# A two-block transformer kernel on one core: one ring of four for all weight halves, context low halves on VectorE, one rounding step on ScalarE

## The chip, the cores and the metric

The kernel runs on one core of a Trainium2 chip, as one program. The metric is the device time of one execution in microseconds; the value before is the median of three runs. The engines are named as in the profile: PE is TensorE (matmuls), DVE is VectorE, ACT is ScalarE, POOL is GpSimd, SP is the engine that issues most of the loads.

## The reference, cut to what matters

Batch 1, 256 tokens, width 1024, all in float32. Two blocks follow each other; the first has two layers, the second one layer.

```python
def reference(x, ...):
    x = first_block(x, ...)      # RWKV-7 mix, SwiGLU; differential attention, SwiGLU
    return second_block(x, ...)  # modulated token mixer, convolutional FFN, final norm

def second_block(x, c, ctx, c_ctx, w_ada, ...):
    ada = silu(c) @ w_ada + b_ada ; ada_c = silu(c_ctx) @ w_ada + b_ada
    hc = modulate(rmsnorm(ctx, norm_mix), csh1, csc1)
    logf_f, k_f, logf_b, k_b, vc = hgrn2_gates(hc @ w_in[:, :3 * w], ...)
    hf_c = advance_state(h0, k_f, vc, ...) ; hb_c = advance_state(h0, flip(k_b), flip(vc), ...)
    h = modulate(rmsnorm(x, norm_mix), sh1, sc1)
    o = token_mixers(h @ w_in, ..., hf_c, hb_c)       # two gated scans and a gMLP branch
    x = x + g1 * (o @ w_out)
    h2 = modulate(rmsnorm(x, norm_ffn), sh2, sc2)
    x = x + g2 * conv_ffn(h2, w_up, taps, conv_b, w_down, rows)   # a * gelu(conv3x3(g))
    return rmsnorm(x, norm_final)
```

The context `ctx` (256 more tokens) is used only for the two start states `hf_c` and `hb_c` of the scans. Three slices of `w_in` are applied to it: the values (`w_iv` in the kernel) and the two gates (`w_cf`, `w_cb`).

## The kernel before, in words

**Products in three parts.** Every large product is made of rounded float32 operands: a value is split into a high half `hi` (the value rounded) and a low half `lo` (what the rounding left), for weights and activations alike. `mm3` then issues three matmuls for each tile, high by high, high by low and low by high. So every weight chunk of 128 rows by 1024 columns is loaded (`raw`, a ring of `NRAW` = 5 buffers, issued by SP), rounded on ACT (`S.copy`, L276) and subtracted (`sub`, L273) before TensorE may use it.

**`stream`** (L279) does that for one chunk. Its `eng` chooses who subtracts: VectorE where nothing is given, GpSimd where `G` is given; with `"dma"` ACT writes the rounded value (L285) and its negative (L286), and a DMA that GpSimd issues (L287) adds the weight from memory onto it. Its `ring` chooses the buffers of the two halves. The usual ring is that of the pool `wp` with `NHI` = 3 pairs, so the rounding of a chunk waits until TensorE is through with the chunk three places earlier in that ring.

**`ptm`** (L377) multiplies tokens by a weight in four chunks of 256 rows each, for both halves of the tokens; `pfm` makes the product with channels on the partitions. The stages, in the order of the program, are: the RWKV projections with a chain over four groups of heads (`p`, `G1`; the time-shifted keys' weight `w_k` is streamed with `"dma"`); the output projection `w_o`; a first feed-forward (`ffn`, 22 steps); key, query and value projections (`pj`); attention in six groups of heads (`heads_a`: scores `sc`, maximum `c_mx`, exponentials `pe`; `heads_b`: the combination of the two softmaxes in `pe`, its transposes `tr`, the product with the values `po`; `heads_c`: the norm of each head and `oT`); the context (below); the attention's output `w_ao`; a second feed-forward; the token mixer (`mh`, gates with `logsig`, eight weights through `pfm` and `ptm`, levels of the scan); `w_out`; and the convolutional feed-forward.

**The context** is normalised in two halves of 128 tokens: the half is loaded into `crow` (a DMA that ACT issues, L1043), its squares are summed on ACT (`sq`, L330), and it is transposed on TensorE by a scaled identity `dg` into a bank `p`, from which `gr`, `chh` and `chl` are made. Then `w_iv` and `w_cf` (beside the attention) and `w_cb` (after `w_ao`) are applied with `ptm`; these three have `lambda m: G`, so GpSimd makes their twelve low halves. The two loads of `ctx` use the same buffer one after the other: in the order of the program the second DMA waits for the last transpose of the first half.

**The mixer's projections** `w_vm`, `w_u`, `w_iv`, `w_ga` are one call of `ptm` with sixteen chunks m. Even chunks have their low half from VectorE and use the ring of three; odd chunks use `"dma"` and a ring `x` of two pairs of their own (tiles `xhi`, `xlo`), so that an odd chunk waits for the chunk four places earlier, an even one for the chunk six places earlier.

**The feed-forward** (`ffn`, L812) prepares the activation of each step in `post`: the hook makes `act`, L833 rounds it to `acth` on VectorE, and `sub` makes `actl` there. The convolutional one (`conv_hook`) uses eight VectorE instructions a step for the taps (L1304), a Gelu on ACT (L1306) and a product (L1307).

**The order of the work** is not that of the text. The whole program is built under `tile.TileContext(nc, schedule_with_timeline_sim=True)` (L1333): a scheduler that imitates the engines' times chooses the order of the instructions on every engine, each of which then runs strictly in its order. Any edit can therefore move instructions far from it.

## Time and profile before

| | us |
|---|---|
| median of three runs | 1212.76 (1209.64 to 1217.07) |
| the profiled execution | 1209.02, its span 1206.9 |
| PE busy | 1113.0, 92% of the span |
| DVE busy | 858.0, 71% |
| ACT busy | 632.5, 52% |
| POOL busy | 194.4, 16% |

The span is the time from the first to the last instruction of the profiled execution; 2.1 us lie around it. Busy time counts the union of an engine's instructions. A busy share is a mean over stages that have different limits: in the three feed-forwards TensorE is busy all the time, in the stages between them it waits. The granted clock of TensorE is given as a share of full speed, so 0.50 is the lower of its two levels (1.2 against 2.4 GHz).

### The profile page before, as it was taken

Reading aid. Unit: us, or ns where it says so; the run is one execution under the profiler, and the core shown is the slowest. Engines: PE = TensorE matmul, PEld = TensorE weight load, DVE = VectorE, ACT = ScalarE, POOL = GpSimd, SP = SyncE. Lnnn points to the kernel's source line nnn. Section 1 sums busy time; section 2 is a strip of 40 time slices with the busy share of each in tenths; the row PEclk is TensorE's granted clock in tenths of the full one; section 3 lists DMA queues with packets and bytes.
Section 4 is the critical chain, followed back from the end, with each engine's and each line's share of the span. In section 5 each row is a group of like instructions: output and inputs, shape, how many; then the busy total and the mean of one; then the engine's idle time right before and its main releaser. Section 6 shows DMA issues by size and latency. Waiting matters only on the chain.

```text
span 1206.9 us, 19872 instructions
## 1 busy us (share of the span) xinstructions
PE 1113.0 (92%) x7788; PEld 975.2 (81%) x7788; DVE 858.0 (71%) x1508; ACT 632.5 (52%) x1042; POOL 194.4 (16%) x156
## 2 busy tenths in 40 slices
PE   4999999779999999998999999999898789999995
PEld 4788549669999998886679999998876669999994
DVE  5687756859997566856659887554667667877787
ACT  6976145445434346757658334444867446344451
POOL 2242301200000001243130000004001112232320
PEclk8989878889999999999999999999989899999998
DMA  5354220248888563544147997662667234555551
GB/s 191 129 133 129 71 62 32 88 146 278 291 271 310 193 210 103 182 158 139 35 158 261 343 329 251 186 209 81 200 183 195 53 122 138 183 185 188 179 158 53
DMA packets 56589, 205.40 MB, mean 170 GB/s; under 512 B 6288, under 2 KB 6800, under 8 KB 56496
## 3 DMA queue, kind: packets, MB, share of 16 engines
q1 hardware_dynamic: 52128, 189.82, 47.0%
q0 software_dynamic: 2016, 7.34, 3.5%
q10 hardware_dynamic: 2352, 6.98, 1.7%
q8 instruction: 61, 1.00, 0.3%
q14 instruction: 32, 0.26, 0.1%
HBM read 203.06 MB, written 1.05 MB: 169 GB/s over the span
## 4 chain that ended last, share of the span: by engine, by line
PE 74%; DVE 12%; ACT 6%; DMA 5%; issue 2%; POOL 1%; POOLq 0%; ACTq 0%; DVEq 0%
PE p L298 31%; PE tr L298 16%; PE acc L298 14%; PE pj L298 6%; PE sc L298 3%; DVE lo L273 1%; DMA raw<-in_dn 1%; PE W L298 1%; ACT hi L276 1%; PE tr L310 1%; PE G L298 1%; PE px L298 1%; DVE cacc L1304 1%; DVE lo L655 1%; DVE lo L657 1%
## 5 line engine op out<-in xcount | busy, mean ns | idle before, releaser
L276 ACT CAST hi<-raw 128x1024 fp32r<-128x1024 f32 x198 | 205.9, 1047 | 153.9 <-PE p L298 84.1
L273 DVE TENSOR_TENSOR lo<-raw,hi 128x1024 fp32r<-128x1024 f32 x162 | 201.9, 1251 | 83.1 <-ACT hi L276 82.9
L298 PE MATMUL p<-fhh,hi 128*128 128x256 f32 x576 | 164.5, 286 | 2.5 <-ACT fhh L276 1.7
L298 PE MATMUL p<-fhl,hi 128*128 128x256 f32 x576 | 165.0, 286 | 1.2 <-DVE fhl L362 0.9
L298 PE MATMUL p<-fhh,lo 128*128 128x256 f32 x576 | 163.9, 285 | 0.0
L276 ACT CAST dhi<-raw 128x1024 fp32r<-128x1024 f32 x66 | 69.2, 1049 | 133.0 <-DMA raw<-in_dn 133.0
L298 PE MATMUL tr<-fhh,hi 128*128 128x256 f32 x480 | 136.0, 284 | 0.0
L298 PE MATMUL tr<-fhl,hi 128*128 128x256 f32 x480 | 135.9, 283 | 0.0
L298 PE MATMUL tr<-fhh,lo 128*128 128x256 f32 x480 | 135.7, 283 | 0.0
L273 DVE TENSOR_TENSOR dlo<-raw,dhi 128x1024 fp32r<-128x1024 f32 x66 | 83.6, 1267 | 56.7 <-ACT dhi L276 56.7
L273 POOL TENSOR_TENSOR lo<-raw,hi 128x1024 fp32r<-128x1024 f32 x36 | 87.8, 2441 | 189.4 <-ACT hi L276 186.0
L298 PEld LDWEIGHTS p<-fhh,hi 128*128 128x128 f32 x576 | 111.4, 193 | 4.5 <-ACT fhh L276 1.9
L298 PEld LDWEIGHTS p<-fhl,hi 128*128 128x128 f32 x576 | 111.3, 193 | 3.5 <-DVE fhl L362 1.7
L298 PEld LDWEIGHTS p<-fhh,lo 128*128 128x128 f32 x576 | 111.3, 193 | 0.3 <-issue 0.2
L298 PE MATMUL acc<-dhi,acth 128*128 128x512 f32 x264 | 103.6, 392 | 1.3 <-DVE acth L833 1.3
L298 PE MATMUL acc<-dlo,acth 128*128 128x512 f32 x264 | 103.4, 392 | 0.0
L298 PE MATMUL acc<-dhi,actl 128*128 128x512 f32 x264 | 100.7, 390 | 1.0 <-DVE actl L273 1.0
L317 POOL TENSOR_TENSOR s_rstd<-s_ms,mhalf 128x1 f32<-128x1 f32 (+2 forms) x32 | 34.8, 1091 | 361.5 <-DVE s_ms L331 272.4
L298 PEld LDWEIGHTS tr<-fhh,hi 128*128 128x128 f32 x480 | 91.9, 192 | 1.2 <-issue 0.2
L298 PEld LDWEIGHTS tr<-fhl,hi 128*128 128x128 f32 x480 | 91.9, 192 | 1.2 <-issue 0.2
L298 PEld LDWEIGHTS tr<-fhh,lo 128*128 128x128 f32 x480 | 91.9, 192 | 0.0
L888 DVE CUSTOM_DVE_ANT_0 junk<-wada,crow 128x1024 f32<-128x1024 f32 x64 | 78.0, 1219 | 8.9 <-DMA wada<-in_w_ada 7.3
(452 smaller groups left out, 2518.5 us busy)
## 6 DMA issues: line engine op xcount, KB each, us to landing
raw<-in_gu SPq DMA_DIRECT2D x132, 512.0 KB, 4.4
raw<-in_dn SPq DMA_DIRECT2D x66, 512.0 KB, 4.4
wada<-in_w_ada SPq DMA_DIRECT2D x48, 512.0 KB, 5.1
raw<-in_w_r SPq DMA_DIRECT2D x8, 512.0 KB, 4.4
raw<-in_w_k SPq DMA_DIRECT2D x8, 512.0 KB, 3.8
raw<-in_w_v SPq DMA_DIRECT2D x8, 512.0 KB, 4.7
raw<-in_w_o SPq DMA_DIRECT2D x8, 512.0 KB, 4.5
raw<-in_w_ak SPq DMA_DIRECT2D x8, 512.0 KB, 4.4
```

The costliest lines, as they stand in the source:

```text
L273: (eng or V).tensor_tensor(out=out, in0=raw, in1=hi.bitcast(F32), op=ALU.subtract)
L276: S.copy(hi, raw)
L298: PE.matmul(out, lhsT=l, rhs=r, start=start, stop=stop, skip_group_check=True)
L310: PE.transpose(o, s_, ident)
L317: G.tensor_tensor(out=r, in0=ms, in1=mhalf[:, :n], op=ALU.pow)
L655: V.tensor_tensor(out=tmp[:, s + 1:, 0:s], in0=bc(Ab[:, s + 1:, s:s + 1], shp), in1=bc(Tb[:, s:s + 1, 0:s], shp), op=ALU.mult)
L657: V.tensor_tensor(out=Tb[:, s + 1:, 0:s], in0=Tb[:, s + 1:, 0:s], in1=tmp[:, s + 1:, 0:s], op=ALU.add)
L888: V.tensor_tensor_reduce(out=junk, in0=raw, in1=src, scale=1.0, scalar=0.0, op0=ALU.mult, op1=ALU.add, accum_out=dst[:, e:e + 1])
L1304: V.scalar_tensor_tensor(out=a4[:, ro, co], in0=g4[:, ri, ci], scalar=taps[:, fb, k:k + 1], in1=a4[:, ro, co], op0=ALU.mult, op1=ALU.add)
```

## The change

`NHI` becomes 4. The ring of four then serves all chunks of the mixer's projections too: the separate ring `x` and the callable form of `ring` are gone, so that every chunk, odd or even, waits for the chunk four places earlier. The three context products lose their `lambda m: G`, which makes VectorE the subtracting engine. In the convolutional feed-forward the rounding of `act` into `acth` is done by ACT, in the two others still by VectorE.

```diff
-NHI = 3
+NHI = 4
...
-        rp, tag, n = ring(i) if callable(ring) else ring or (wp, "", NHI)
+        rp, tag, n = ring or (wp, "", NHI)
...
-            V.tensor_copy(ah, raw)
+            (S.copy if hook is conv_hook else V.tensor_copy)(ah, raw)
...
+    conv_hook = None
...
-    ptm([(a["w_iv"], 0, lambda t, ps: S.copy(cv[:, t * 512:(t + 1) * 512], ps))], ch, 0, lambda m: G)
+    ptm([(a["w_iv"], 0, lambda t, ps: S.copy(cv[:, t * 512:(t + 1) * 512], ps))], ch, 0)
...
-        ptm([(w, 0, got.__setitem__)], ch, 0, lambda m: G, acc_bank=acc_bank)
+        ptm([(w, 0, got.__setitem__)], ch, 0, acc_bank=acc_bank)
...
-        eng=lambda m: "dma" if m % 2 else V, ring=lambda i: (MX, "x", 2) if i % 2 else (wp, "", NHI))
+        eng=lambda m: "dma" if m % 2 else V)
```

The line numbers after L861 are two higher in the changed kernel. Since the scheduler makes the order, the edit shows itself in many places of the engines' queues. Three of them follow.

ACT, where the second half of the context is loaded (`crow_5541`; `pj`, `qsq` and the `hi` of L292 belong to the key, query and value projections). Before:

```order
L292 ACTIVATE hi_4721<-raw_4719,cst_67 128x512 x2
L1043 DMA crow_5541<-in_ctx 128x1024
L330 ACTIVATE sq_5543,s_ss_5544<-crow_5541 128x512
L292 ACTIVATE hi_4736<-raw_4734,cst_67 128x512 x2
L276 CAST chh_5501<-gr_5534 128x4x128
L330 ACTIVATE sq_5543,s_ss_5544<-crow_5541 128x512
L932 ACTIVATE qsq_4655<-pj_4566 128x512
```

Changed (L956 became L958; `pe_5154` and `pe_5155` are the first exponentials of the attention):

```order
L954 ACTIVATE av_4462<-pj_5094,rx_4424 128x512
L958 ACT_TABLE_LOAD
L276 CAST hi_5635<-raw_5633 128x1024
L356 ACTIVATE gr_5522<-p_5517,adc_2280,gm_2281 128x128 x4
L1045 DMA crow_5541<-in_ctx 128x1024
L330 ACTIVATE sq_5543,s_ss_5544<-crow_5541 128x512
L276 CAST chh_5500<-gr_5522 128x4x128
L276 CAST chh_5501<-gr_5534 128x4x128
L330 ACTIVATE sq_5543,s_ss_5544<-crow_5541 128x512
L980 ACTIVATE pe_5154,c_se_5151<-sc_5148,c_mx_5150 128x128 x4
L980 ACTIVATE pe_5155,c_se_5151<-sc_5149,c_mx_5150 128x128 x4
```

The second half's load stood in the middle of the projections; now it stands behind them, directly ahead of the attention's first exponentials.

PE, the start of the attention (`sc` are the scores, `tr_5213` the first transposes of `pe`; `p_5583`, `p_5590` and `p_5661` are context projections, `p_5553` and `p_5565` transposes of the context). Before, the end of that piece:

```order
L298 MATMUL p_5590<-hi_5635,chl_5503 128x512
L298 MATMUL p_5590<-hi_5635,chh_5501 128x512
L298 MATMUL p_5590<-lo_5636,chh_5501 128x512
L298 MATMUL sc_5177<-kT_4458,qT_4460 128x128 x4
L298 MATMUL sc_5178<-kT_4458,qT_4460 128x128 x4
L310 MATMUL tr_5213<-cst_67,pe_5154 128x128 x4
L298 MATMUL p_5590<-hi_5635,chl_5503 128x512
L298 MATMUL p_5661<-hi_5657,chh_5500 128x512
```

Changed:

```order
L298 MATMUL pj_5094<-hi_5103,xnl_4395 128x512
L298 MATMUL p_5517<-dg_5515,crow_5505 128x128
L298 MATMUL p_5529<-dg_5515,crow_5505 128x128 x4
L298 MATMUL sc_5148<-kT_4457,qT_4459 128x128 x4
L298 MATMUL sc_5149<-kT_4457,qT_4459 128x128 x4
L298 MATMUL sc_5177<-kT_4458,qT_4460 128x128 x4
L298 MATMUL p_5553<-dg_5551,crow_5541 128x128 x4
L298 MATMUL p_5565<-dg_5551,crow_5541 128x128 x4
L298 MATMUL sc_5178<-kT_4458,qT_4460 128x128 x4
L310 MATMUL tr_5213<-cst_67,pe_5154 128x128 x4
L298 MATMUL p_5583<-hi_5579,chh_5500 128x512
```

Before, 47 of the 48 matmuls of the first context product stood between the end of the projections and `tr_5213`; now none does, and thirteen of the sixteen transposes of the context stand behind the projections.

ACT in the mixer, around the last of the four `logsig` chains (`ls_8486`; `hi_8558` and `hi_8588` are chunks of `w_q`, 9026 and 9058 the first two odd chunks, `hi_9013` the first even one). Before:

```order
L285 CAST xhi_9026<-raw_9024 128x1024
L276 CAST hi_8558<-raw_8556 128x1024
L1031 ACTIVATE ls_8486<-p_8425 128x512
L286 ACTIVATE xlo_9027<-xhi_9026 128x1024
L1036 ACTIVATE kb_8215<-ls_8418 128x512
L1032 ACTIVATE ls_8486<-ls_8486 128x512
L285 CAST xhi_9058<-raw_9056 128x1024
L276 CAST hi_8588<-raw_8586 128x1024
L1033 ACTIVATE ls_8486<-ls_8486 128x512
L286 ACTIVATE xlo_9059<-xhi_9058 128x1024
```

Changed:

```order
L276 CAST hi_8588<-raw_8586 128x1024
L1033 ACTIVATE ls_8486<-p_8425 128x512
L1234 COPY grow_9331<-sp_9374 128x512
L1034 ACTIVATE ls_8486<-ls_8486 128x512
L1035 ACTIVATE ls_8486<-ls_8486 128x512
L276 CAST hi_9013<-raw_9011 128x1024
L1137 ACTIVATE qe_8660<-gb_8214 128x512
L1038 ACTIVATE kb_8215<-ls_8486 128x512
L285 CAST hi_9026<-raw_9024 128x1024
L1132 COPY ke_8659<-kf_8213 128x512
L1114 COPY qc_8216<-p_8493 128x512
L1133 COPY ke_8659<-kb_8215 128x512
```

The odd chunks' copies stood between the steps of the chain; now the chain comes first and the odd chunks follow it.

## Rows read from the trace of the kernel before

**Rows 1.** The page, engines: busy us (share of the span) and instructions.

```profile
PE 1113.0 (92%) x7788; PEld 975.2 (81%) x7788; DVE 858.0 (71%) x1508; ACT 632.5 (52%) x1042; POOL 194.4 (16%) x156
```

**Rows 2.** Windows by stage: length, busy us of each engine, PEclk, DMA share, GB/s.

```profile
534.00:560.00 26.00, 24.12 (x125) 18.99 (x124) 13.55 (x23) 17.66 (x52) 16.28 (x7) 1.00 0.39 129
560.00:600.00 40.00, 35.26 (x181) 25.76 (x181) 26.84 (x67) 26.78 (x81) 4.30 (x6) 0.96 0.18 58
...
870.00:930.00 60.00, 51.97 (x578) 41.70 (x579) 43.66 (x59) 41.55 (x59) 5.22 (x6) 0.86 0.68 186
```

**Rows 3.** Timeline of POOL and DVE beside the attention: start, us, instruction, [idle before].

```profile
546.02 4.72 POOL L273 TENSOR_TENSOR lo<-raw,hi 128x1024 fp32r<-128x1024 f32 x2 [4.03 <-ACT hi L276]
...
545.54 5.36 DVE L989 SCALAR_TENSOR_TENSOR pe<-pe,c_cf,pe 128x128 f32<-128x128 f32 x4
...
556.66 1.14 DVE L989 SCALAR_TENSOR_TENSOR pe<-pe,c_cf,pe 128x128 f32<-128x128 f32 x4
...
617.85 2.42 DVE L340 TENSOR_SCALAR dg<-cst,s_rstd 128x128 f32<-128x128 f32 x1 [0.67 <-POOL s_rstd L317]
```

**Rows 4.** The page, costliest groups: busy us, mean ns, idle before.

```profile
L273 DVE TENSOR_TENSOR lo<-raw,hi 128x1024 fp32r<-128x1024 f32 x162 | 201.9, 1251 | 83.1 <-ACT hi L276 82.9
...
L273 POOL TENSOR_TENSOR lo<-raw,hi 128x1024 fp32r<-128x1024 f32 x36 | 87.8, 2441 | 189.4 <-ACT hi L276 186.0
```

**Rows 5.** Timeline of ACT, projections and start of the attention.

```profile
470.95 1.50 ACT L356 ACTIVATE gr<-p,adc,gm 128x128 f32<-128x128 f32 x4 [1.49 <-PE p L298]
...
478.32 0.33 ACTq L1043 DMA_DIRECT2D crow<-in_ctx  x1
483.05 0.63 ACT L330 ACTIVATE sq<-crow 128x512 f32<-128x512 f32 x1 [4.05 <-DMA crow<-in_ctx]
...
534.85 1.28 ACT L956 ACT_TABLE_LOAD   x1
...
542.11 0.37 ACT L978 ACTIVATE pe<-sc,c_mx 128x128 f32<-128x128 f32 x1 [3.98 <-DVE c_mx L974]
```

**Rows 6.** Timeline of PE, context transposes and the attention.

```profile
477.46 0.83 PE L298 MATMUL p<-dg,crow 128*128 128x128 f32 x6
...
537.32 1.71 PE L298 MATMUL sc<-kT,qT 64*128 64x128 f32 x16
...
550.95 0.33 PE L310 MATMUL tr<-cst,pe 128*128 128x128 f32 x1 [1.88 <-DVE pe L989]
...
572.01 1.16 PE L298 MATMUL po<-av,pT 128*128 128x128 f32 x8 [2.44 <-ACT pT L992]
```

**Rows 7.** PE in the mixer: two waits of the timeline, then two windows with PEclk.

```profile
862.89 0.36 PE L298 MATMUL p<-mhh,hi 128*128 128x256 f32 x1 [0.91 <-DVE ls L1035]
872.36 0.55 PE L298 MATMUL p<-mhh,hi 128*128 128x256 f32 x1 [3.63 <-DVE ls L1035]
...
874.00:876.00 2.00, 2.00 (x11) 0.50 1.05 381
...
878.00:880.00 2.00, 2.00 (x19) 1.00 0.73 248
```

**Rows 8.** The mixer's odd chunks: ACT's timeline, and the chain of waits.

```profile
892.37 1.03 ACT L285 CAST xhi<-raw 128x1024 fp32r<-128x1024 f32 x1
...
910.68 8.52 DMA xlo<-in_w_iv
```

**Rows 9.** Timeline of PE in the RWKV stage.

```profile
62.99 0.58 PE L298 MATMUL p<-xkh,lo 128*128 128x256 f32 x1 [3.24 <-DMA lo<-in_w_k]
```

**Rows 10.** Timeline of PE at the output projection `w_o` and in the tail.

```profile
235.71 0.63 PE L310 MATMUL tr<-cst,Y 128*128 128x128 f32 x4 [1.47 <-DVE Y L795]
...
1191.62 0.50 PE L298 MATMUL acc<-dhi,acth 128*128 128x512 f32 x1 [1.31 <-DVE acth L833]
```

**Rows 11.** Timeline of POOL in the projections, the small powers.

```profile
477.71 2.01 POOL L317 TENSOR_TENSOR s_rstd<-s_ms,mhalf 128x8 f32<-128x8 f32 x1 [1.01 <-DVE s_ms L322]
...
491.64 1.64 POOL L317 TENSOR_TENSOR s_rstd<-s_ms,mhalf 128x8 f32<-128x8 f32 x1 [0.70 <-DVE s_ms L322]
```

## The prediction, made before the changed kernel was run

> **What bounds the kernel now.** I read the page's engines first: TensorE is busy for 1113.0 of 1206.9 us [rows 1], so no edit to another engine can give more than the 94 us in which it waits, and what counts is which waits go and which come. The windows by stage say where they are: none in the feed-forwards, 1.9 us in the first 26 us of the attention and 4.7 in the next 40, 8.0 in the 60 us of the mixer from 870 on [rows 2]. Then the timeline, for what ends each wait. Two things are to be seen there. GpSimd's low halves take 2.44 us each against 1.25 on VectorE [rows 4], and while GpSimd makes them some VectorE instructions stretch: four combinations of the softmaxes took 5.36 us beside two of them and 1.14 us without, the scaled identity `dg` 2.42 us [rows 3]. [...]
>
> **The change, part by part.** Since the scheduler reorders everything, I count stage by stage what TensorE waits for, with the changed queues as they will run.
>
> *Attention and context, +5 us (-1 to +9).* Twelve low halves leave GpSimd (12 x 2.44 = 29.3 us) and VectorE gets 12 x 1.25 = 15.0 us, which it has: it is busy 13.6 of 26 and 26.8 of 40 us there. The gain is the holds: 5.36 - 1.14 = 4.2 us at 545.54, which TensorE felt as the 1.88 us at 550.95 [rows 3, 6]. The loss is the order. Before, the load of the second context half was issued at 478.32, and ACT stood still for 4.05 us until it landed at 483.05 [rows 5]; the projections filled TensorE meanwhile, so it cost nothing. Now it is issued behind the projections, because the transposes of the first half, for whose buffer it waits, moved there, and the attention's first exponentials are queued behind it on ACT. From the end of the projections: a copy of about 0.6 (as the 0.63 of `sq`), the table load 1.28, a rounding of 1.05 (the 1.03 of `xhi` [rows 8]) and four `gr` 1.50 make 4.4; the DMA 483.05 - 478.32 = 4.7 makes 9.2; two `sq` and two `chh`, 4 x 0.63, make 11.7; eight exponentials at 0.34 (the 0.37 at 542.11, overlapping) 14.4; on VectorE two small steps and the combination, 0.4 + 1.14, 16 us. TensorE has for that span only the scores, 2 x 1.71, and thirteen transposes, 26 records at 0.83/6 = 3.6 us [rows 5, 6]: 7 us, so it waits about 9. Before, 47 context matmuls stood there. They come later now, between the groups, and fill waits like the 2.44 us at 572.01; of the 4.7 us of 560 to 600 I leave 2. So 9 + 2 against 1.9 + 4.7 gives +4.4, and a clock that falls once at least, as it did at 572 too (PEclk 0.96 in that stage), +0.6. The ends: +9 if the later waits all stay (+2.7) and the low clock costs 2 us more than now, -1 if ACT gets through its queue 5 us sooner than I add up, with the load landing while TensorE still has projections.
>
> The reverse hold is in this too: GpSimd's small powers ran 2.01 us at 477.71, beside VectorE's work on weights, and 1.64 us at 491.64 [rows 11], so 0.4 for each of the six powers of the attention, 2 us at most, mostly hidden by the context matmuls. The Trainium skill (SBUF — State Buffer, "Who interferes with whom") says that a VectorE instruction with two SBUF inputs and a GpSimd instruction that reads SBUF shut each other out for the whole of the one that came first. By that rule the new low halves could hold each power for up to 1.25 us, 7.5 us for six, and if all of it were on the path the sum below would be +3 instead of -4.5 and the time 1216; the two rows show a hold of about the rest of a running VectorE instruction, which bears the rule out in kind, at a third of that size.
>
> *Start of the second feed-forward, -1 us (-3 to 0).* The low halves of `w_cb` held `dg` twice, 2.42 us against 0.3 for an undisturbed one (4.2 us for both, estimated by the one row [rows 3]); TensorE had `w_cb`'s own matmuls meanwhile, so little of it shows.
>
> *Mixer, -8 us (-13 to +2).* Before, the copies of the odd chunks lay on ACT between the steps of the last `logsig` chains, whose end frees the bank TensorE wants: waits of 0.91 and 3.63 us, and then half clock from 872.4 to about 877, 2.3 us more [rows 7]. In the new order absolute value, exponential and logarithm follow each other, and by the durations of before the bank is free about 1 us ahead of TensorE: -6.8 us. Against this the first odd chunk now shares the ring and is rounded only when the first product of `w_q` is through: two copies and three smaller steps, some 4 us, then a DMA like the 8.52 us at 910.68 [rows 8], say 7.5, makes 11.5; TensorE comes to it after 48 matmuls of 256 columns at 0.117 (19 in the 2.00 us from 878 on, some of them shorter [rows 7]) and 14 of 512 at twice that, 8.9 us: a wait of about 2.5. Further on, the odd chunk of `w_u` was rounded at 892.37 behind a copy that waited for TensorE, a table load and two exponentials; now it stands ahead of them, and by the same sums its low half lands some 9 us earlier, that of `w_iv` too. I count 4 us of that, since VectorE (43.7 of 60 us busy) has to follow [rows 2]: -6.8 + 2.5 - 4 = -8. All of it would give -13. The other end is a wait of 2.5 us at each of the four weights, 10 - 6.8 = +3, less 1 for `w_u`. The ring itself is neutral: an odd chunk waited for the one four places earlier before, and an even one, which now does too, is ready 6 us sooner than its odd neighbour anyway.
>
> *RWKV, +0.5 us (-4 to +4).* TensorE waits 3.24 us for a low half that comes by DMA [rows 9]. ACT, full there, now rounds one chunk more (1.05 us) ahead of that chunk's second copy, and earlier chunks sooner: the two small waits ahead shift into this one. The exponentials of the chain come later, but TensorE has 38 more matmuls ahead of `G1`.
>
> *`w_o`, -1 us (-2.5 to +1.5).* A fourth chunk is ready and its 24 matmuls stand ahead of the transposes that waited 1.47 us [rows 10].
>
> *Convolutional feed-forward, 0 (-1 to +1.5).* VectorE loses 22 roundings, but TensorE never waits in the loop; the cover is its own work. In the tail it waits 1.31 us for the last `acth` [rows 10], and ACT is a few tenths slower on that shape.
>
> The sum is 5 - 1 - 8 + 0.5 - 1 + 0 = -4.5 us: 1209.0 of the profiled execution becomes 1204.5. That execution is 3.7 us below the median of its three runs, so as a median **1208 us**, 0.4% less, which is not to be told from no change: about 1% is what a measurement of this kernel can tell.
>
> **The rivals.** *The first exponentials are not held up, and the mixer gives all it can.* The load would land early enough, or ACT's queue move faster, so that the attention gives -1 instead of +5 and the mixer -13: the sum is -15.5, 1197 us, 1.3% faster. For it: the waits that go are in the trace, those that come are my addition. Against: ACT's wait for this load is in the trace, and only the projections hid it.
>
> *The single ring makes the odd chunks late: slower.* Place: the first odd chunk of each of the four mixer weights. Each wait of 2.5 us, and the half clock behind it (2.3 us, as at 872), is 4.8; four are 19, less 6.8 for the bank's waits, +12 for the mixer; with the attention's +5 and the rest at -1.5 the sum is +16, 1228 us, 1.3% slower. It decides from the point where a DMA'd half lands over 2 us behind TensorE's wish at every weight. For it: such halves took up to 8.52 us to land. Against: in the order before they were issued later for three of the four.
>
> *The change does nothing measurable*, because the weight stream was never what TensorE waited for and the reordering cancels out: 1213, inside the forecast.
>
> **How the numbers follow.** No change within 1% (the forecast and the third rival, own range 1201 to 1219): 0.53. The first rival, and what lies near it below 1200.6: 0.32. The slower one, above 1224.9: 0.15. The range for 8 in 10 leaves one in ten out on either side: it goes into the first rival, to 1194, and to 1224 above, where the attention's +9 and the mixer's +2 come together: 1212.8 + 9 + 2.
>
> **What the changed profile would show.** A wait of TensorE of 7 to 10 us near 540, ahead of the first `tr`, with ACT standing some 4 us for `crow` right before the first `pe`; no wait over 1 us in 560 to 600 on `po`; `pe` at 1.1 to 1.5 us for four; no low half on POOL in the attention; no wait on `ls` in the mixer, one of 1 to 4 us on the first `lo` of `w_vm`, and the last product of the mixer ending 8 to 13 us sooner against its start. The prediction is wrong if the first of these is missing, or if the mixer's odd chunks wait at every weight.

## The result, and the profile after

The changed kernel takes 1220.08 us (median of 20 runs, 1213.97 to 1223.51), the kernel before 1211.26 in the same comparison (20 runs): a ratio of 1.007, 95% interval 1.0054 to 1.0085. It is slower by some 8.5 us, inside the forecast range of 1194 to 1224, but on the other side of zero than the forecast of -4.5 us. The range was wide enough to hold a wrong sign, so that is no support for the forecast. Its profiled execution has a span of 1216.6 us, 9.7 more than before.

The page, engines (as [rows 1]). TensorE's own work is the same; it is busy 5 us longer at a lower clock, and waits 4 us more.

```profile
PE 1118.4 (92%) x7788; PEld 978.6 (80%) x7788; DVE 873.3 (72%) x1498; ACT 642.6 (53%) x1066; POOL 164.3 (14%) x144
```

The windows of [rows 2], of the changed kernel: attention, its second part, mixer. They lie at the same times as before, while the changed kernel enters the attention 2.6 us and the mixer 11.6 us later, so a row compares nearly, and not exactly, the same work.

```profile
534.00:560.00 26.00, 17.88 (x100) 15.58 (x99) 14.29 (x35) 17.32 (x54) 0.55 (x1) 0.80 0.31 101
560.00:600.00 40.00, 38.75 (x188) 28.24 (x187) 30.19 (x71) 30.02 (x86) 4.11 (x5) 1.00 0.33 106
870.00:930.00 60.00, 56.75 (x694) 45.95 (x697) 46.77 (x64) 49.94 (x70) 6.12 (x7) 1.00 0.78 206
```

In the first row TensorE is busy 6.2 us less and has 0.20 less of clock; in the other two it is busy 3.5 and 4.8 us more and, in the mixer, has 0.14 more of clock. The big wait is where the forecast put it. PE's timeline of the changed kernel there, then ACT's:

```profile
547.62 2.07 PE L298 MATMUL sc<-kT,qT 64*128 64x128 f32 x8 [8.12 <-ACT pe L980]
```

```profile
537.49 1.28 ACT L958 ACT_TABLE_LOAD   x1
538.79 0.33 ACTq L1045 DMA_DIRECT2D crow<-in_ctx  x1
...
543.81 0.63 ACT L330 ACTIVATE sq<-crow 128x512 f32<-128x512 f32 x1 [2.58 <-DMA crow<-in_ctx]
...
546.09 0.35 ACT L980 ACTIVATE pe<-sc,c_mx 128x128 f32<-128x128 f32 x1
```

TensorE stood for 8.12 us while ACT issued the load of the second context half, waited 2.58 us for it (some 4 were forecast) and only then came to the first exponential.

To see where the 9.7 us arose I cut each profile at five points: the last `G` of RWKV, the last `acc` of the first and of the second feed-forward, the norm of the last feed-forward (its first `dg`), and its last `acc`. The table gives how much longer than before each piece is, with all kernels of the experiments. One row is one profile, so a small number in it is not a result; the ratios come from the timed runs. Some profiled executions lie far from the median of their kernel: those of mixer_order_alone and four_in_mixer_conv_vector 8.5 and 6.5 us above it, those of three_to_w_o and conv_no_pool 4.3 and 3.1 us below. How far a piece moves without any edit in it can be read in the mixer column: conv_only, ctx_only and ctx_cb_on_pool have the mixer's order of before and stand at -2.6, +0.1 and -1.1.

| kernel | RWKV | `w_o`, 1st ff | attention to 2nd ff | mixer, `w_out` | last ff | ratio (95% interval) |
|---|---|---|---|---|---|---|
| changed kernel | +4.2 | +1.3 | +6.1 | -8.6 | +6.7 | 1.007 (1.0054 to 1.0085) |
| conv_only | +0.4 | -0.2 | +5.0 | -2.6 | +2.3 | 1.0027 (1.0009 to 1.0045) |
| ctx_only | -0.8 | -0.2 | +6.6 | +0.1 | +0.7 | 1.0045 (1.0025 to 1.0064) |
| ring_only | +4.8 | +0.8 | +7.1 | -11.0 | +9.9 | 1.0119 (1.0089 to 1.0148) |
| all_but_conv | +3.3 | +1.1 | +6.2 | -8.3 | +12.5 | 1.0123 (1.0095 to 1.015) |
| conv_no_pool | +1.6 | 0.0 | +6.0 | -8.1 | -1.0 | 1.0007 (0.9983 to 1.0031) |
| ctx_own_buffer | +3.0 | +3.2 | +8.3 | -9.1 | +7.2 | 1.0076 (1.0046 to 1.0107) |
| rwkv_exp_first | +5.2 | +1.3 | +7.8 | -8.0 | +5.7 | 1.0095 (1.0061 to 1.0129) |
| mixer_order_alone | +0.7 | +2.1 | +3.7 | -4.1 | +2.3 | 0.9949 (0.9925 to 0.9974) |
| mixer_ring_of_three | -0.8 | +0.3 | +3.8 | -1.5 | -0.4 | 1.0009 (0.9984 to 1.0035) |
| ctx_cb_on_pool | -0.8 | 0.0 | +3.3 | -1.1 | +0.7 | 0.9997 (0.9972 to 1.0022) |
| ctx_and_mixer | +0.1 | +0.9 | +3.3 | -4.1 | +0.9 | 1.0011 (0.9983 to 1.0038) |
| rwkv_k1_vector | +1.9 | +1.3 | +6.9 | -9.0 | +6.8 | 1.0028 (1.0001 to 1.0055) |
| three_to_w_o | +0.2 | -2.3 | +6.8 | -10.4 | +4.4 | 1.001 (0.9991 to 1.0028) |
| four_in_mixer | +0.6 | +1.5 | -0.2 | -9.5 | +9.9 | 1.0029 (1.001 to 1.0049) |
| four_in_mixer_conv_vector | +1.2 | +1.9 | +3.5 | -4.0 | -0.1 | 0.996 (0.9937 to 0.9984) |
| both_steps_undone | -0.6 | -3.6 | +9.6 | -9.1 | -0.1 | 0.9969 (0.9952 to 0.9985) |

The forecast by the same pieces was +0.5, -1, +4, -8 and 0. The mixer's sum is right; RWKV and the last feed-forward are not.

### The profile page after: what moved, and what is told of

Its sections match the earlier page's. It is cut to its first block, busy times and chain, and to the rows that moved or that the text cites. A ratio compares the mean times of both kernels' runs of the same rounds, so it can differ in the third digit from the quotient of the medians.

```text
span 1216.6 us, 19906 instructions
## 1 busy us (share of the span) xinstructions
PE 1118.4 (92%) x7788; PEld 978.6 (80%) x7788; DVE 873.3 (72%) x1498; ACT 642.6 (53%) x1066; POOL 164.3 (14%) x144
## 3 DMA queue, kind: packets, MB, share of 16 engines
HBM read 203.06 MB, written 1.05 MB: 168 GB/s over the span
## 4 chain that ended last, share of the span: by engine, by line
PE 73%; DVE 12%; DMA 6%; ACT 6%; issue 2%; POOL 0%; ACTq 0%; POOLq 0%; DVEq 0%
PE p L298 31%; PE tr L298 15%; PE acc L298 12%; PE pj L298 6%; DMA raw<-in_dn 3%; PE sc L298 3%; DVE cacc L1306 2%; PE W L298 1%; PE tr L310 1%; ACT hi L276 1%; DVE lo L273 1%; PE G L298 1%; PE px L298 1%; DVE actl L273 1%; DVE lo L655 1%
## 5 line engine op out<-in xcount | busy, mean ns | idle before, releaser
L273 DVE TENSOR_TENSOR lo<-raw,hi 128x1024 fp32r<-128x1024 f32 x174 | 213.1, 1229 | 95.2 <-ACT hi L276 94.3
L273 DVE TENSOR_TENSOR dlo<-raw,dhi 128x1024 fp32r<-128x1024 f32 x66 | 80.7, 1223 | 44.8 <-ACT dhi L276 44.5
L273 POOL TENSOR_TENSOR lo<-raw,hi 128x1024 fp32r<-128x1024 f32 x24 | 59.8, 2490 | 154.2 <-ACT hi L276 142.5
```

The costliest lines, as they stand in the source:

```text
L273: (eng or V).tensor_tensor(out=out, in0=raw, in1=hi.bitcast(F32), op=ALU.subtract)
```

## The experiments

**The parts of the change, one by one.** The rounding on ACT alone, in the kernel before:

```diff
-            V.tensor_copy(ah, raw)
+            (S.copy if hook is conv_hook else V.tensor_copy)(ah, raw)
```

> The kernel before with one part of the change: the rounding of the convolutional activation on ScalarE. The order of all engines is that of before up to the convolutional stage. Theory: the low half of the activation now waits for ScalarE and comes late by some 0.3 us in about half of the 22 steps, so the loop's acc matmuls wait on actl: +3 us in that stage, nothing elsewhere, about +0.25%. Rival: the loop is bound by TensorE and hides it, and the 6.7 us that the changed kernel loses in this stage come from the clock at its start (0.79 there against 0.91): then 0 us here.

1212.82 us against 1208.69. The last feed-forward is 2.3 us longer, near the theory's 3, but the profile does not decide between the two: from the first product of the stage to its first `acc` the granted clock was 0.93 over 22.8 us where before had 1.00, which alone makes some 1.6 us. The 5 us in the attention are not the edit's, since no instruction moved there (see the last section).

The context's low halves on VectorE alone (and the same for `w_iv`):

```diff
-        ptm([(w, 0, got.__setitem__)], ch, 0, lambda m: G, acc_bank=acc_bank)
+        ptm([(w, 0, got.__setitem__)], ch, 0, acc_bank=acc_bank)
```

> The kernel before with one part of the change: the twelve low halves of the context on VectorE. The second load of the context stays in the middle of the projections. Theory: with the holds by GpSimd gone (4.2 us on pe, 4.2 us on dg), the wait of 1.88 us at the first transposes of the attention shrinks and those of the later groups with it: -4 us (-2 to -8) between the end of the projections and the second feed-forward, nothing elsewhere. Rival: the 15 us more on VectorE lengthen the chain of every group: +2 us or more.

1213.85 us, slower where -4 was expected. A gain up to the last transposes of `pe` is there (they are 2.0 us sooner in its profile, 1.0 of it from ahead of the attention), and was lost behind them: the first transposes of the second feed-forward's norm are 5.2 us late, and the later ones wait 4.82 us for `fhl`.

The single ring of four alone:

```diff
-NHI = 3
+NHI = 4
...
-        eng=lambda m: "dma" if m % 2 else V, ring=lambda i: (MX, "x", 2) if i % 2 else (wp, "", NHI))
+        eng=lambda m: "dma" if m % 2 else V)
```

> The kernel before with the ring of four for all chunks, context low halves still on GpSimd, rounding still on VectorE. Theory: the ring alone moves the orders: RWKV and w_o +5 us (as in the changed kernel), attention +4 to +8 (the second context load behind the projections, and GpSimd's holds as well), mixer -8, convolutional stage 0 to +3: together +3 us (0 to +8). Rival: the moved context load is due to the context's new engine, and the attention is unchanged here: then -3 us.

1223.13 us, the slowest but one. The ring by itself costs 14 us where 0 to 8 were expected; it holds the mixer's gain and also most of the losses, and the last feed-forward, expected at 0 to +3, is the largest with +9.9.

The changed kernel with `acth` back on VectorE:

```diff
-            (S.copy if hook is conv_hook else V.tensor_copy)(ah, raw)
+            V.tensor_copy(ah, raw)
```

> The changed kernel with the rounding of the convolutional activation back on VectorE. Theory: 3 us less than the changed kernel in the convolutional stage (no waits on actl), so +6 us against the kernel before. Rival (the clock at the start of the stage): the same as the changed kernel, +9 us against before.

1223.51 us, against both expectations: beside the ring of four the rounding on ACT saves some 6 us of the last feed-forward (12.5 against 6.7), while alone it cost. What it meets there is the next point.

**The last feed-forward.** Timelines of VectorE and GpSimd in one step: the kernel before, the changed one, and all_but_conv.

```profile
1100.61 2.48 POOL L273 TENSOR_TENSOR lo<-raw,hi 128x1024 fp32r<-128x1024 f32 x1 [6.25 <-ACT hi L276]
1100.75 1.76 DVE L1304 SCALAR_TENSOR_TENSOR cacc<-tr,cst,cacc 128x189 f32<-128x189 f32 x4
...
1103.52 0.29 DVE L833 CAST acth<-act 128x256 fp32r<-128x256 f32 x1
1103.84 0.43 DVE L273 TENSOR_TENSOR actl<-act,acth 128x256 fp32r<-128x256 f32 x1
```

```profile
1104.83 2.49 POOL L273 TENSOR_TENSOR lo<-raw,hi 128x1024 fp32r<-128x1024 f32 x1 [6.41 <-ACT hi L276]
...
1105.64 1.96 DVE L273 TENSOR_TENSOR actl<-act,acth 128x256 fp32r<-128x256 f32 x1
```

```profile
1105.35 2.50 POOL L273 TENSOR_TENSOR lo<-raw,hi 128x1024 fp32r<-128x1024 f32 x1 [6.70 <-ACT hi L276]
1105.50 2.50 DVE L833 CAST acth<-act 128x256 fp32r<-128x256 f32 x1
```

Before, GpSimd's low half lay beside the taps (`cacc`, which read a bank) and held nothing. In the order of a ring of four it starts just as VectorE comes to `acth` or, where ACT rounds, to `actl`, and that instruction ends with GpSimd's: 2.50 us for 0.29, 1.96 for 0.43. To test whether this makes the loss, GpSimd's halves were taken away in the changed kernel:

```diff
-        lambda f: G if f else V)
+        lambda f: V)
```

> The changed kernel with one more edit: in the convolutional feed-forward all low halves of the weights are made by VectorE, none by GpSimd. Theory (the 6.7 us that the changed kernel loses in that stage are VectorE held by GpSimd: `actl` 1.96 us beside a low half of GpSimd, 0.43 before): `actl` comes back to 0.43 to 0.5 us, TensorE's waits for it go, and the stage from the first `acc` to the last gets 3 to 6 us shorter than in the changed kernel: 1214 to 1217 us where that one has 1220. Rival (VectorE has no room: 22 low halves of 1.25 us on top of its own work fill its steps of 8.5 us, and `actl` queues behind them): `actl` is short, but TensorE waits for low halves or for `actl` as before, and the time is within 2 us of the changed kernel's, or above it.

1210.79 us, level with before; the last feed-forward is 7.7 us shorter than in the changed kernel. Groups of VectorE from 1040 to 1165 us (busy, mean ns, idle before), the changed kernel and this one:

```profile
L273 DVE TENSOR_TENSOR actl<-act,acth 128x256 fp32r<-128x256 f32 x15 | 26.8, 1787 | 0.0
```

```profile
L273 DVE TENSOR_TENSOR actl<-act,acth 128x256 fp32r<-128x256 f32 x16 | 6.6, 415 | 0.0
```

And the window 1040 to 1165 of before, the changed kernel, this one and all_but_conv:

```profile
1040.00:1165.00 125.00, 125.00 (x881) 117.64 (x880) 100.21 (x193) 55.02 (x74) 37.52 (x15) 1.00 0.57 183
```

```profile
1040.00:1165.00 125.00, 123.55 (x851) 113.11 (x850) 110.53 (x171) 57.93 (x85) 34.98 (x14) 1.00 0.56 179
```

```profile
1040.00:1165.00 125.00, 125.00 (x872) 117.18 (x871) 110.19 (x198) 61.96 (x90) 0.00 (x0) 1.00 0.57 185
```

```profile
1040.00:1165.00 125.00, 121.36 (x836) 112.34 (x834) 117.76 (x173) 52.78 (x70) 34.89 (x14) 0.99 0.54 169
```

VectorE is as busy in the third (110.19) as in the second (110.53), yet TensorE no longer waits: the same busy time was work in the one and standing in the other. TensorE's busy time shows only 1.45 us of the changed kernel's loss in this window. Counted in columns (a matmul has 256 or 512) it got through 271,104 in this window before, 262,656 in the changed kernel, 271,104 in this one and 256,512 in all_but_conv, at a clock of 0.99 to 1.00: at 0.118 us for 256 columns the changed kernel is 3.9 us behind and all_but_conv 6.7. Another part of the 6.7 us of the whole piece is the clock at its start: from the first product to the first `acc` 0.88 was granted over 22.7 us, where before had 1.00 and this kernel 0.94. The theory held, the rival (no room on VectorE) fell; the time fell below the 1214 to 1217 that were expected. The same edit in the kernel before was not run, so it stays open how much of the gain is more than the loss undone.

**The load in front of the exponentials.** The changed kernel with the second context half in a buffer of its own:

```diff
-        cx = DP("crow", 1024, 2)
+        cx = DP("crow", 1024, 2) if t == 0 else CX("crow1")
```

> The changed kernel with one more edit: the second half of the context rows is loaded into a buffer of its own, so that its load does not wait for the transposes of the first. Theory (the wait of 8.12 us ahead of the attention's first `tr` is ACT standing for that load): the load is issued early, ACT does not stand for `crow`, and the wait falls to 3 to 4 us; with what the clock gives back the time is 4 to 7 us under the changed kernel's, 1213 to 1216 us. Rival (the wait is the length of the chain of ACT and VectorE behind the projections, and the load runs beside it): the wait stays at 6 us or more and the time within 2 us of the changed kernel's.

PE's waits ahead of the first `tr` of the attention in this kernel:

```profile
542.05 1.16 PE L298 MATMUL p<-dg,crow 128*128 128x128 f32 x8 [0.70 <-ACT gr L356]
545.30 0.80 PE L298 MATMUL p<-hi,chh 128*128 128x512 f32 x1 [2.09 <-ACT gr L356]
```

The wait fell from 8.12 to 2.8 us, as the theory said, but the time did not move: 1220.04 us where 1213 to 1216 were expected. The order changed with it; waits of 1.93 and 1.18 us came at 585 to 588, with a clock of 0.56 at 590 to 600, and the piece is 8.3 us longer than before instead of 6.1. So the load makes the wait, but taking the wait away did not shorten the kernel.

**RWKV.** In the changed kernel ACT's timeline ahead of the first exponentials reads:

```profile
57.99 1.07 ACT L286 ACTIVATE lo<-hi 128x1024 fp32r<-128x1024 f32 x1
58.94 1.06 ACT L276 CAST hi<-raw 128x1024 fp32r<-128x1024 f32 x1
59.87 1.08 ACT L286 ACTIVATE lo<-hi 128x1024 fp32r<-128x1024 f32 x1
60.83 0.91 ACT L568 ACTIVATE sqk<-k,cst 128x256 f32<-128x256 f32 x2
...
65.46 0.64 ACT L544 ACTIVATE e<-cs 128x512 f32<-128x512 f32 x1
```

and PE's waits there:

```profile
61.40 0.59 PE L298 MATMUL tr<-cst,sqk 128*128 128x2 f32 x2 [2.10 <-ACT sqk L568]
65.43 0.58 PE L298 MATMUL p<-xkh,lo 128*128 128x256 f32 x1 [3.44 <-DMA lo<-in_w_k]
```

The first `e` came at 59.58 before, so it is 5.9 us late, and the 3.24 us of [rows 9] are still there (3.44) with 2.10 more. Windows of PE (length, busy us, granted clock, DMA share, GB/s), before and in the changed kernel:

```profile
60.00:65.00 5.00, 2.01 (x9) 0.69 0.42 81
65.00:70.00 5.00, 5.00 (x32) 0.62 0.08 30
```

```profile
60.00:65.00 5.00, 0.59 (x2) 0.57 0.70 125
65.00:70.00 5.00, 4.57 (x21) 0.50 1.03 272
```

First I put the roundings behind the exponentials by hand:

```diff
-            wh, wl = stream(w, 2 * i + f, 8, eng(f))
+            with behind(late if f else {}):
+                wh, wl = stream(w, 2 * i + f, 8, eng(f))
...
+            exped = mark("Activation")
...
+            with behind(exped if fp else {}):
+                proj_r(fp + 2)
```

(`late` is `exped` for the second `w_k`.)

> The changed kernel with one more edit: in RWKV the rounding of the second chunk of the second `w_k`, and those of the last `w_r`, are put behind the first exponentials on ACT, where they stood before. Theory (the 4.2 us that the changed kernel loses by the last `G` are the four roundings and copies that the fourth buffer lets ACT do ahead of `sqk` and of the exponentials, 65.46 us against 59.58): the exponentials come back to 59 to 60 us, the wait of 2.1 us for `sqk` goes, the last `G` is 2 to 4 us sooner than in the changed kernel, and the time 2 to 4 us shorter, 1216 to 1218. Rival (the halves that come by DMA set the pace, with 3.24 us of wait before and 3.44 after): the rounding put off makes that wait longer by what the chain gains, and the last `G` stays within 1 us of the changed kernel's.

1220.84 us, nothing gained. PE's timeline:

```profile
64.26 0.58 PE L298 MATMUL p<-xkh,lo 128*128 128x256 f32 x1 [4.99 <-DMA lo<-in_w_k]
81.24 0.58 PE L298 MATMUL p<-xkh,lo 128*128 128x256 f32 x1 [4.17 <-DMA lo<-in_w_k]
```

The exponentials came back to 61.34 and the first `G` to 71.63 (77.01 in the changed kernel), but the halves that come by DMA are waited for 9.2 us. That is the rival's result. Then the DMA was taken away at that weight:

```diff
-        ps = pfm(a["w_k"], fp, xk, lambda f: "dma" if fp else None)
+        ps = pfm(a["w_k"], fp, xk, lambda f: "dma" if fp > 1 else None)
```

> The changed kernel with one more edit: the low halves of the second `w_k` in RWKV are made by VectorE instead of by a DMA behind a negative copy on ACT. Theory (in RWKV ACT's queue and the halves that come by DMA trade places: what is put ahead of the exponentials delays the chain, what is put behind them delays the halves, as the run with the exponentials first showed: 9.2 us of wait for the halves): with two negative copies less on ACT (2 x 1.08 us) the exponentials come some 2 us sooner, no wait for a half by DMA remains at the second `w_k`, and the last `G` is 2 to 5 us sooner than in the changed kernel, level with before; 1215 to 1218 where the changed kernel has 1220. Rival (VectorE, busy 13 to 17 of 20 us there, gets two low halves of 1.25 us and hands the delay on to `BK`): the wait for the halves goes and one for `BK` or `lo` of the same length comes, with the last `G` within 1.5 us of the changed kernel's.

1213.15 us. The wait for the halves is gone, two for `RB` came (2.67 and 0.67 us), and the last `G` is 2.3 us sooner: the ratio agrees with the theory's sign and more than its size, while the profile alone would not decide it.

Last, the whole effect of the fourth buffer was removed from this stage. One place of the ring is filled at the start and read again during `w_o`; until then the order on every engine is that of before, instruction by instruction, but for the two fills on GpSimd. (`hold()` is called right behind its definition; `release` copies eight columns of both tiles.)

```diff
+    def hold():
+        for tag in ("hi", "lo"):
+            t_ = wp(tag, 1024, NHI, F32R)
+            G.memset(t_[:, :8].bitcast(F32), 0.0)
+            held.append(t_)
...
+    with behind(mark()):
+        release()
```

> The changed kernel, in which one place of the ring of four is kept occupied from the start to the end of `w_o`, so that RWKV and `w_o` run in the order of before. Theory (the fourth buffer lets ACT round two chunks and make a negative copy ahead of the first exponentials, and the whole chain behind them is late): the first `G` comes at 68.5 to 70.5 us, the last at 131 to 134, the norm of the first feed-forward at 258 to 261 us, and the time is 3 to 5 us shorter than the changed kernel's, 1215 to 1217. Rival (the loss is the clock of those profiles and not the order): the waits are those of before, but the time is within 1.5 us of the changed kernel's, 1218.5 to 1221.5.

1211.76 us. ACT's timeline again, for the lines shown of the changed kernel:

```profile
55.97 1.07 ACT L286 ACTIVATE lo<-hi 128x1024 fp32r<-128x1024 f32 x1
56.92 0.92 ACT L582 ACTIVATE sqk<-k,cst 128x256 f32<-128x256 f32 x2
58.34 1.28 ACT L558 ACT_TABLE_LOAD   x1
59.64 0.63 ACT L558 ACTIVATE e<-cs 128x512 f32<-128x512 f32 x1
```

By the ratios (1.007 to 1.001) this gives back 7 us, more than was expected: RWKV is level, and `w_o`, where the fourth buffer does come, gains 2.3 us instead of losing 1.3. Over all profiles, eleven with the order of before end RWKV at -0.8 to +1.2 us (mean 0.0), five with the full ring of four at +1.6 to +4.8 (mean 3.4).

**The mixer.** The order without the ring, in the kernel before:

```diff
+    gated = mark("Activation")
...
+    with behind(gated):
         ptm([(w, 0, ...
```

> The kernel before, with rings as they were, and one edit: the four mixer weights are issued behind the last step of the last `logsig` chain on ACT, so that no copy of an odd chunk stands between the chain's steps. Theory (the mixer's 8.6 us came from the order on ACT, not from the ring): no wait of TensorE for `ls`, 1.00 granted at 870 to 880, the mixer's last product 6 to 10 us sooner than before, and the time 5 to 8 us shorter, 1201 to 1206 where before has 1209. Rival (the fourth buffer of the single ring let the odd chunks of `w_u` and `w_iv` come in time): the waits for `ls` go, but as much comes back as waits for `xhi` or `xlo` at the first odd chunks, and the time is within 3 us of before.

1204.90 us, faster than both kernels, as the theory said. The waits for `ls` shrink from 4.8 to 1.1 us, and a wait for `xlo` comes: 2.8 us at `w_vm`. In its profile, its slowest execution (1213.41), the stage gains 4.1 us where 6 to 10 were expected. Then the ring without the fourth buffer:

```diff
-        eng=lambda m: "dma" if m % 2 else V, ring=lambda i: (MX, "x", 2) if i % 2 else (wp, "", NHI))
+        eng=lambda m: "dma" if m % 2 else V)
```

> The kernel before with one edit: the odd chunks of the mixer's four weights share the ring of the even ones, which keeps its three buffers. Theory (half of the mixer's gain is the order on ACT, and the rest is that the odd chunks are rounded where the single ring puts them, for which three buffers are enough): from the mixer's norm to the norm of the last feed-forward 7 to 10 us less than before, as in the kernels with a ring of four (8.1 to 10.9), against 4.1 with the order alone; 1200 to 1204 us where before has 1209. Rival (it takes the fourth buffer, so that a chunk is ready ahead of TensorE): each even chunk now waits for the odd one three places earlier, waits for `lo` by DMA come at most weights, and the stage gains 0 to 4 us; 1206 to 1211.

1210.56 us against 1210.54, inside the rival's 1206 to 1211. PE's waits at the first odd chunk of the four weights, in the kernel before (none at `w_vm`), in this kernel, then in the changed one:

```profile
900.72 0.80 PE L298 MATMUL p<-xlo,mhh 128*128 128x512 f32 x1 [0.58 <-DMA xlo<-in_w_u]
...
919.24 0.79 PE L298 MATMUL p<-xlo,mhh 128*128 128x512 f32 x1 [3.31 <-DMA xlo<-in_w_iv]
...
934.04 0.50 PE L298 MATMUL p<-xlo,mhh 128*128 128x512 f32 x1 [1.44 <-DMA xlo<-in_w_ga]
```

```profile
884.27 0.79 PE L298 MATMUL p<-lo,mhh 128*128 128x512 f32 x1 [2.89 <-DMA lo<-in_w_vm]
...
903.96 0.63 PE L298 MATMUL p<-lo,mhh 128*128 128x512 f32 x1 [2.74 <-DMA lo<-in_w_u]
...
920.53 0.50 PE L298 MATMUL p<-lo,mhh 128*128 128x512 f32 x1 [1.49 <-DMA lo<-in_w_iv]
...
936.06 0.50 PE L298 MATMUL p<-lo,mhh 128*128 128x512 f32 x1 [0.42 <-DMA lo<-in_w_ga]
```

```profile
888.14 0.50 PE L298 MATMUL p<-lo,mhh 128*128 128x512 f32 x1 [0.41 <-DMA lo<-in_w_vm]
...
902.34 0.50 PE L298 MATMUL p<-lo,mhh 128*128 128x512 f32 x1 [1.62 <-DMA lo<-in_w_u]
...
918.51 0.50 PE L298 MATMUL p<-lo,mhh 128*128 128x512 f32 x1 [0.40 <-DMA lo<-in_w_iv]
...
933.52 0.50 PE L298 MATMUL p<-lo,mhh 128*128 128x512 f32 x1 [2.93 <-DMA lo<-in_w_ga]
```

With three buffers the forecast's 2.5 us stand at `w_vm` and `w_u`. In the changed kernel the first three waits are together 4.7 us shorter, and that at `w_ga` is 2.5 us longer. Over the four weights the changed kernel waits 5.4 us, as the kernel before did (5.3), and this one 7.5. The reverse, in ring_only's kernel, with `hold` as above: before's order up to the mixer's norm, and four places in the mixer alone:

```diff
         normT(xres[t], t, gain_ev(mh, gm[:, 0], ada[:, 0:8]))
+    with behind(mark()):
+        release()
...
         eng=lambda m: "dma" if m % 2 else V)
+    hold()
```

> The kernel before with a ring of four for all chunks in the mixer alone: one place is kept occupied up to the mixer's norm and again behind its last weight; context and convolution as before. Theory (the mixer's gain of 8 to 11 us is the order on ACT, some 4, plus the fourth buffer, with which the odd chunks come in time; the rest of the change only costs): from the mixer's norm to the last feed-forward's norm 7 to 11 us less than before, waits for `lo` under 2 us at `w_vm`, `w_u` and `w_iv`, and 1200 to 1204 us where before has 1210. Rival (the mixer's gain in the changed kernel came from its different state at the mixer's start, 10 us later with other chunks already rounded): the stage gains 0 to 4 us, and the time is 1206 to 1211.

The mixer gains 9.5 us, as expected (though the wait at `w_u` is 2.87 us, where under 2 was), and the kernel is slower than either expectation, 1214.00 us: its last feed-forward takes 9.9 us longer, with `acth` at 2.34 us a piece between 1040 and 1165. The shifted order put GpSimd beside `acth` there too, though the ring of three was back. With that removed:

```diff
-    hold()
...
-            V.tensor_copy(ah, raw)
+            (S.copy if hook is conv_hook else V.tensor_copy)(ah, raw)
...
-        lambda f: G if f else V)
+        lambda f: V)
```

> The kernel just named, with the ring of four kept to the end, all low halves of the convolutional feed-forward on VectorE and its activation rounded by ACT. Theory (without GpSimd's holds the order of a ring of four costs nothing in that stage): the stage from its norm to its last `acc` takes 196 to 199 us, as before (198.6) and without GpSimd's halves (197.6), and the time is within 2 us of the kernel just named. Rival (VectorE, which then makes all halves, is too full at the start of the stage, where TensorE first asks for them): the stage takes 201 us or more, and the time is 3 us or more above the kernel just named.

1204.71 us, 9 below the kernel just named; the stage is level with before. The expectation of equal times was wrong, since the kernel it was measured against had a hold of its own.

**The start of the second feed-forward.** The context on VectorE, `w_cb` on GpSimd:

```diff
-        ptm([(w, 0, got.__setitem__)], ch, 0, lambda m: G, acc_bank=acc_bank)
+        ptm([(w, 0, got.__setitem__)], ch, 0, (lambda m: G) if w is a["w_cb"] else (lambda m: None), acc_bank=acc_bank)
```

> The kernel before with the low halves of `w_iv` and `w_cf` made by VectorE, those of `w_cb` by GpSimd as before. Theory (the loss at the start of the second feed-forward, +2.8 from the last matmul of `w_ao` to the norm and 4.8 us of wait for `fhl` when all three are on VectorE, is that `w_cb`'s matmuls, whose low halves are then ready early, run in a block ahead of the norm's transposes and no longer fill the norm's waits): with `w_cb` slow again its matmuls stand between the transposes, the wait for `fhl` falls to 2 us or less, and the stage up to the last `acc` of the second feed-forward is within 1.5 us of before; 1207 to 1210 where before has 1209. Rival (the loss is the order up to the end of `w_ao`, where the attention's groups end later): the wait shrinks but the last `acc` stays 4 us or more late, 1212 to 1215.

1209.90 against 1210.54 us. The wait for `fhl` fell from 4.82 to 0.9 us and the piece, one profile each, by 3.3 us against ctx_only. Together with the mixer on a ring of three:

> The two edits just named together: `w_iv` and `w_cf` on VectorE, and the mixer's four weights on the single ring of three. If the two stages are independent, the time is that of before plus what each gives alone: by the theories of the two runs 1198 to 1203 us, by their rivals 1209 to 1216.

1211.40 us: neither edit had gained, nor do both; that the two would add up was not put to a test by edits that gain nothing.

**Both failed steps taken out**: the edit of three_to_w_o in the changed kernel, and with it:

```diff
-        lambda f: G if f else V)
+        lambda f: V)
```

> The changed kernel with both edits: one place of the ring kept occupied to the end of `w_o`, and no low half on GpSimd in the convolutional feed-forward. Theory (the two losses are separate): the sum of what each gave back, 8 and 9 us, 1202 to 1206 us where before has 1210 and the changed kernel 1220; the stage of the last feed-forward 196 to 199 us. Rival (what is gained early is lost again later, as in the kernel with the ring of four in the mixer alone, whose last feed-forward took 208 us): 1209 to 1213, no better than each edit alone.

1205.64 us, 0.9969 of before. By the ratios 12 us come back of the 15 that the two gave apart; the attention of its profile is longer (+9.6 against +6.8 in three_to_w_o), so some of it may be lost there.

## Why the prediction was wrong

*RWKV, +0.5 forecast, +4.2 measured: the step that failed.* The working said that the small waits ahead would shift into the wait of [rows 9], and that the late exponentials would be covered by 38 matmuls ahead of `G1`. The cover held: the first `G` is 6.7 us late, but TensorE does not wait for it. The small waits are gone too (0.72 and 1.05 us). What failed is the count of ACT's work. One rounding more was counted; three `hi`, a `lo` (4.2 us), a copy and a `kp` (1.2 us) stand ahead of `e` that stood behind it before. `sqk` stands behind part of them, and TensorE waits 2.10 us for it, a term that the sum did not have, while the wait for the DMA'd half stays. TensorE's idle time up to the last `G` grows by 2.1 us. The other 2.1 are longer busy time at a lower clock (granted 0.57 and 0.50 from 60 to 70 us for 0.69 and 0.62), which the forecast had put at nothing here. The chain and the DMA'd halves share ACT, so what one wins the other loses (rwkv_exp_first), and of the kernels tried only those with the order of before are level (three_to_w_o).

*The last feed-forward, 0 forecast, +6.7 measured: the other step that failed.* "TensorE never waits in the loop; the cover is its own work" was nearly true of the order before (1.0 us of wait in all, for `actl`). That GpSimd's twenty-two low halves held nothing there was read as a property of the stage, where it was their place beside `cacc`. The holds had been priced for the attention from [rows 3] (5.36 against 1.14, 2.42 for `dg`) and were not asked for here. They make most of the loss, and the lower clock at the stage's start is in it too. The Trainium skill (SBUF — State Buffer, "Who interferes with whom") says that a cast that can use both ports, or a VectorE instruction with two inputs in SBUF, and a GpSimd instruction that reads SBUF shut each other out for the whole instruction, and that a VectorE instruction with at most one SBUF input, outside the modes that use both ports, does not. The traces agree: `acth` 2.50 for 0.29, `actl` 1.96 for 0.43, `cacc` unchanged at 0.43.

*`w_o`, -1 forecast, +1.3 measured.* With RWKV in its old order the gain is there, -2.3 and -3.6 in two profiles; in the changed kernel it is not. Why the late RWKV takes it away was not tried.

*Attention and the second feed-forward's start, +4 forecast, +6.1 measured.* The mechanism is right, term by term: 8.12 us of wait for about 9, ACT standing for `crow`, one wait over 1 us on `po` (1.08) for none. The reverse hold did not come: the six powers of the attention took 0.69 to 1.02 us, as before (0.70 to 1.01). The rows it was read from were misread: a power's time goes with its width, 0.55 us for one column, 0.70 for two, 1.01 for four and 1.64 for eight, so the 1.64 us of [rows 11] was no hold, and of the 2.01 at most 0.4. Mis-sized was the start of the feed-forward, -1: it is +2.6 (from the last `w_ao` to the last `acc`, +9.0 to +11.6). The step saw that `w_cb`'s matmuls covered the held `dg`, but not that it was GpSimd's slowness that kept them there; with quick halves they run ahead as a block, and the norm is left with a wait of 4.07 us for `fhl`. ctx_cb_on_pool shows that in the order of before.

*The mixer, -8 forecast, -8.6 measured.* Right in sum, and in part by luck. The bank's term came: no wait for `ls` is left of 4.8 us. The two terms of the odd chunks did not, and cancelled: the first of them waits 0.41 us where 2.5 was counted, and of the 4 us that `w_u` and `w_iv` were to give back, 1.9 came and `w_ga` took 1.5 (2.93 for 1.44). A wait for a copy on ACT (`vu`, 1.79 us at 897.42) shrank to 0.29 as well, which no term had. There is a wait at every weight, three of them under 2 us, which the prediction had named as a sign of being wrong. mixer_order_alone (-4.1) and the rings of three (-1.5, -4.1) against eleven profiles with four (-4.0 to -11.0, mean -8.6) suggest about half for the order and half for the fourth buffer. But profiles with the order of before spread from -2.6 to +0.1, and four_in_mixer and four_in_mixer_conv_vector, whose order is the same up to the end of the mixer, are 5.5 us apart in it, so the split is not shown.

*The rivals.* The slower one was to come from late odd chunks in the mixer, with 2.5 us at each weight. Its direction was right and its place wrong: in the changed kernel only the wait at `w_ga` is that long, and the four together are no longer than before.

## What to carry to other kernels

When a scheduler sets the order, a deeper ring is not one edit but a new order in every stage it serves: price each, and where a stage loses keep a place of the ring occupied there, which isolates the effect and gave the time back. Where a slow engine shares an access with a fast one, ask not whether they collide now but what keeps them apart; if it is only the order, the next edit anywhere ahead can end it, as four_in_mixer showed without touching the stage. A wait that is removed (8.12 to 2.8 us) need not shorten anything: follow the piece to its end. And where a piece's sum comes out, compare its terms too: two that are wrong can cancel.

## What the runs showed that was not expected

The same instructions in the same order took some 62.5 or some 67.5 us from the end of the last projection to the end of the last transposes of `pe`: before and four_in_mixer the first (62.6, 62.5), conv_only, mixer_order_alone, mixer_ring_of_three and four_in_mixer_conv_vector the second (67.1 to 68.3). The waits are alike (1.88 and 2.44 us before, 1.89 and 2.45 in conv_only); what the clock does after them is not. Windows of before and of conv_only:

```profile
570.00:580.00 10.00, 6.93 (x19) 3.32 (x20) 8.40 (x22) 7.50 (x27) 1.71 (x2) 0.83 0.15 52
580.00:590.00 10.00, 8.75 (x61) 6.99 (x60) 6.45 (x20) 6.91 (x23) 0.70 (x1) 1.00 0.00 0
```

```profile
570.00:580.00 10.00, 6.54 (x23) 3.17 (x20) 7.85 (x20) 8.76 (x30) 1.71 (x2) 0.73 0.20 68
580.00:590.00 10.00, 10.00 (x39) 6.86 (x38) 4.16 (x9) 3.69 (x11) 0.00 (x0) 0.59 0.00 0
```

The profile that the prediction was made from had the quick one, so part of the +6.1 in the attention is what before itself shows in four of six profiles of that order. What decides it was not found. The length of the wait alone does not: behind the 1.88 us at 550.95 before had a clock of 1.00, and conv_only 0.50 for the first 2 us behind its 1.89 us.
